# Standing the three-pass expert chunks in blocks of their own, in a two-layer diffusion backbone on one core

## The chip, the cores and the metric

One of the cores of a Trainium2 chip runs the whole program. Its engines are TensorE (PE, with its weight loads PEld), VectorE (DVE), ScalarE (ACT), GpSimd (POOL) and SyncE (SP, which here issues the loads). Each engine takes its own instructions in a fixed order and waits for the others by semaphores. The metric is device microseconds of one execution; lower is better.

## The reference, cut to what matters

Two layers work on 256 latent and 256 context tokens of width 1024. Layer 0 is a gated MLP mixer and a dense SwiGLU, layer 1 a recurrent mixer and a mixture of experts. The change touches the experts alone:

```
logits = hf @ w_router                        # 256 tokens, 8 experts
top_val, top_idx = lax.top_k(logits, 2)
probs = softmax(top_val)
combine = sum(one_hot(top_idx, 8) * probs[..., None], axis=1)
for e in range(8):
    out = out + combine[:, e:e+1] * ((silu(hf @ w_gate[e]) * (hf @ w_up[e])) @ w_down[e])
```

Here w_gate and w_up are 1024 x 3584 and w_down 3584 x 1024 for each expert, all float32: 352 MB for the eight.

## The kernel before, in words

All weights come from HBM once, in blocks of 128 x 2048 (1 MB), by one queue on SP, into 13 buffers in the expert stage. A load starts when its buffer is free, in the order in which the chunks stand in the program.

The tokens are routed on the chip, and the experts 1 to 7 are ranked by how many tokens chose them. Rank 1, 2 and 3 make lane 0, and expert 0 and the ranks 7, 6, 5, 4 make lane 1 (`moe_regions`, lines 162 to 187). An expert's hidden width of 3584 is cut into 7 chunks of 512. A chunk takes 6 blocks: two of gate, two of down (of an earlier chunk of the expert, since the down product needs the gated result) and two of up. Chunks of the lanes alternate in a fixed list.

Ranks 1 and 2 (`THREE`, line 159) are the fullest. Their chunks run in `whole` (lines 1370 to 1394), with the weights as the moving operand in three passes: each quarter of a block, a piece, is rounded on ACT (the cast, L1354), the rest is taken on DVE (the subtraction, L1355), and PE multiplies three times (L528, L529, L530). There are 24 pieces in a full chunk, so 72 matmuls, and four pairs of buffers (`whp`, `wlp`) for pieces; `prep` (lines 1363 to 1368) makes pieces ahead, four of them before the chunk begins. For the down product the hidden tile is first transposed on PE (L1379) and split by ACT and DVE (L1380, L1381). The silu stands in L1392 and the product with up in L1394.

All other chunks run in `chunk` (lines 1327 to 1347), in float32 without rounding, in an arm chosen by the number of tokens. I call these the side chunks. In such a chunk PE transposes the hidden tile (L1332), ACT copies it (L1333), PE does gate (L1314), down (L1341) and up (L1314), and ACT and DVE sum partial results in a chain (`total`, L1320 to L1324, then L1336 and L1347). Tokens of an expert beyond 128 go through the same chunk again in the over block (`over`, lines 1404 to 1417, entered by the test at L1456). When an expert is done, its rows are scattered back into the tokens (`scatter`, L1400).

The order on each engine is made by a scheduler. It may mix the instructions that stand in the program between tests. What stands inside a tested block (`tc.If`) it places as one piece. In the kernel before, the side chunks and the over blocks are such pieces, and `whole` stands outside of any (line 1443).

Of the kernel before, what the change touches and what calls it, by code (L numbers as in the profile page):

```python
# [158 lines left out]
THREE = (1, 2)  # L159
# [33 lines left out]
def region_slots(op):  # L193
    kind, r, c = op
    out = []
    for w in "gdu":
        cc = c - LAG[r] if w == "d" else c
        if 0 <= cc < NCH:
            out += [(r, cc, w, i) for i in range(2)]
    return out  # L200
# [90 lines left out]
def block_kernel(ctx, tc, xin, pos, cst, rows, wsT, adaS, adaT, wA, lruG, wr, wM, out):  # L291
# [235 lines left out]
    def mm3(o, lh, ll, rh, rl, start, stop):  # L527
        PE.matmul(o, lh, rh, start=start, stop=False)  # L528
        PE.matmul(o, lh, rl, start=False, stop=False)  # L529
        PE.matmul(o, ll, rh, start=False, stop=stop)  # L530
# [796 lines left out]
    def chunk(U, n, bt, bg, bu, yb_, raws, first, last, hd, hw, hook=None):  # L1327
        rg, rd, ru = raws
        m = P // n
        if rd:  # L1330
            for kk in range(4):
                PE.transpose(bt[:, kk * m:(kk + 1) * m], hd[0:m, kk * P:(kk + 1) * P], ident[0:m, 0:m])  # L1332
            ACT.copy(U.th[:, 0:4 * m], bt[:, 0:4 * m])  # L1333
        if rg:
            proj(bg, U.x, rg, n)
            ACT.activation(hw[0:m], total(bg, n), AF.Silu)  # L1336
        if rd:
            for kk in range(4):
                r, g = divmod(kk, n)
                for hf in range(2):  # L1340
                    PE.matmul(yb_[hf][m * g:m * g + m], U.th[:, kk * m:(kk + 1) * m], rd[hf][1][:, kk * 512:(kk + 1) * 512],  # L1341
                              start=(first and r == 0), stop=(last and r == 4 // n - 1), **tp(n, g))
        if rd and hook is not None:
            hook()
        if ru:
            proj(bu, U.x, ru, n)
            DVE.tensor_mul(hw[0:m], hw[0:m], total(bu, n))  # L1347
# [3 lines left out]
    def piece(key, kk, n):  # L1351
        raw = st.peek(key)[:, kk * 512:(kk + 1) * 512]
        wh, wl = wp[0][:, n % 4], wp[1][:, n % 4]
        ACT.copy(wh, raw)  # L1354
        DVE.tensor_tensor(out=wl, in0=raw, in1=wh.bitcast(F32), op=ALU.subtract)  # L1355
        return wh, wl
# [3 lines left out]
    def pieces(op):  # L1360
        return [(k, kk) for k in region_slots(op) for kk in range(4)]

    def prep(op, n):
        got = ahead.setdefault(op, [])
        ps = pieces(op)
        while len(got) < min(n, len(ps)):
            got.append(piece(*ps[len(got)], cnt[0]))
            cnt[0] += 1

    def whole(E, op, bt, bg, bu):  # L1370
        c = op[2]
        hw = hsel(E, c, E.hh)[1]
        prep(op, 4)
        ps = pieces(op)
        xh, xl_ = E.base.x
        yb_ = E.base.y
        if any(k[2] == "d" for k, _ in ps):
            for kk in range(4):
                PE.transpose(bt[:, kk * P:(kk + 1) * P], hw[:, kk * P:(kk + 1) * P], ident)  # L1379
            ACT.copy(thl[0], bt)  # L1380
            DVE.tensor_tensor(out=thl[1], in0=bt, in1=thl[0].bitcast(F32), op=ALU.subtract)  # L1381
        for n, ((_, _, w, i), kk) in enumerate(ps):
            wh, wl = ahead[op][n]
            kb = 4 * i + kk
            if w == "d":
                q = slice(kk * P, (kk + 1) * P)
                mm3(yb_[i], thl[0][:, q], thl[1][:, q], wh, wl, c == 1 and kk == 0, c == NCH and kk == 3)
            else:
                mm3(bg if w == "g" else bu, xh[:, kb], xl_[:, kb], wh, wl, kb == 0, kb == 7)
            prep(op, n + 5)  # L1390
            if w == "g" and kb == 7:
                ACT.activation(hw, bg, AF.Silu)  # L1392
            if w == "u" and kb == 7:
                DVE.tensor_mul(hw, hw, bu)  # L1394

    def scatter(GT, src):
        for hf in range(2):
            for t in range(2):
                b = nb[0]()
                PE.matmul(b, GT[:, t * P:(t + 1) * P], src[:, hf * 512:(hf + 1) * 512], start=True, stop=True)  # L1400
                a = acc[:, t, hf * 512:(hf + 1) * 512]
                DVE.tensor_add(a, a, b)

    def over(E, c, n, raws):
        U = E.over
        p0, p1 = bks[2 * par[0]:2 * par[0] + 2]
        first = c == LAG[E.e]
        yb_ = [p0, p1]

        def keep():  # L1410
            for hf in range(2):
                yc = U.y[:, 512 * hf:512 * hf + 512]
                if first:
                    DVE.tensor_copy(yc, yb_[hf])
                else:
                    DVE.tensor_add(yc, yc, yb_[hf])  # L1416
        chunk(U, n, p0, p1, p0, yb_, raws, True, True, *hsel(E, c, E.oh), keep)

    def hsel(E, c, hh):
        lag = LAG[E.e]  # L1420
        c += NCH * E.n
        return hh[(c - lag) % lag], hh[c % lag]

    def region(E, op, raws):
        c = op[2]
        p0, p1 = bks[2 * par[0]:2 * par[0] + 2]
        lag = LAG[E.e]
        a = (p1, p0, p1, E.base.y, raws, c == lag, c == NCH + lag - 1, *hsel(E, c, E.hh))

        def few_():  # L1430
            if E.e == 3:
                with tc.If(E.rl > 32) as c2:
                    chunk(E.base, 4, *a)
                with c2.Else():
                    chunk(E.base, 2, *a)
                return
            with tc.If(E.rv > 32) as c2:
                chunk(E.base, 2, *a)
            with c2.Else():
                chunk(E.base, 4, *a)  # L1440

        if E.e in THREE:
            whole(E, op, p1, p0, p1)
        elif E.e == 3:
            with tc.If(E.rl > 0) as c1:
                few_()
            with c1.Else():
                chunk(E.base, 1, *a)
        else:
            with tc.If(E.rv > 64) as c1:  # L1450
                chunk(E.base, 1, *a)
            with c1.Else():
                few_()
        if E.e >= 4:
            return
        with tc.If(E.ro > 0):  # L1456
            with tc.If(E.ro > 32) as c3:
                over(E, c, 1, raws)
            with c3.Else():
                over(E, c, 4, raws)  # L1460
# [3 lines left out]
    E = exps[0]  # L1464
# [65 lines left out]
    def start(E):  # L1530
        E.over = over_st[E.s, E.n % 2]
        E.oh = hu[E.s]
        E.base.y = ((y0, y1), (y2, y3))[E.s]
        gather_over(E)
# [3 lines left out]
    def yrot(E):  # L1538
        def f():
            cyc[0] += 1  # L1540
            return E.base.y[cyc[0] % 2]
        return f
    parts = {}
    runs = [o for o in regs if o[0] in "RF"]
    for kind, e, c in regs:
        if kind == "O":
            exps[e] = Expert(e, Qr)
            parts[e] = gather_parts(exps[e])
            parts[e][0]()
        elif kind == "G":  # L1550
            for f in parts[e][1:]:
                f()
            start(exps[e])
        elif kind == "S":
            E = exps[e]
            nb[0] = yrot(E)
            scatter(E.base.GT, Ys[E.s])
            if e < 4:
                with tc.If(E.ro > 0):
                    DVE.tensor_scalar(E.over.y, E.over.y, E.over.ps, None, op0=ALU.mult)  # L1560
                    scatter(E.over.GT, E.over.y)
            nb[0] = rot
        else:
            E = exps[e]
            par[0] ^= 1
            op = (kind, e, c)
            n = runs.index(op)
            if n + 1 < len(runs) and e not in THREE and runs[n + 1][1] in THREE:
                prep(runs[n + 1], 4)
            keys = region_slots(op)  # L1570
            rg, rd, ru = [[(None, st.peek(k)) for k in keys if k[2] == w] or None for w in "gdu"]
            region(E, op, (rg, rd, ru))
            rg, rd, ru = [st.take_raw([k for k in keys if k[2] == w]) for w in "gdu"]
            for r in (rg, rd, ru):
                if r:
                    st.free(r)
            if kind == "F" and c == NCH + LAG[e] - 1:
                ACT.activation(Ys[E.s][:, 0:512], E.base.y[0], AF.Copy, scale=E.base.ps)
                DVE.tensor_scalar(Ys[E.s][:, 512:1024], E.base.y[1], E.base.ps, None, op0=ALU.mult)
# [38 lines left out]
```

## Time and profile before

| | us |
|---|---|
| median of 3 runs (lowest, highest) | 1915.27 (1914.77, 1919.74) |
| the profiled execution: its own time | 1919.62 |
| its span, from the first to the last instruction | 1917.8 |
| PE busy | 1669.5 (87%) |
| DVE busy | 1063.2 (55%) |
| ACT busy | 768.6 (40%) |
| loads: 489 MB read, mean over the span | 256 GB/s |

The span has three parts. Up to about 860 us runs all but the experts, with PE busy in nearly every slice. From 895 to 1599 us the chunks of rank 1 and 2 alternate with side chunks, and PE's busy share falls to seven or eight tenths. After 1599 us rank 3 and the last ranks of lane 1 run. The profile's times come from one execution; a wait named there is put down to what released it last. "PEq" or "DVEq" with a line is the sequencer at a branch.

### The profile page before, as it was taken

What the parts mean: (1) busy time and instruction counts of PE and PEld (TensorE: products, weight loads), DVE (VectorE), ACT (ScalarE), POOL (GpSimd) and SP (SyncE); (2) the same over time, 40 slices, a digit from 0 to 9 for tenths busy, and PEclk for the clock granted to TensorE, in tenths of its full rate; (3) what the DMA queues carried; (4) which work ended last, traced back from release to release, by engine and by line L of the source; (5) the groups of instructions that cost most, each with busy time, mean ns of one, the idle gap of its engine ahead of it and who ended that gap; (6) DMA issues with size and microseconds to landing.
All of it is one profiled execution on the core that took longest, in us unless ns stands there. A gap on an engine that the chain in (4) does not pass through costs nothing. (4 is left out here: it accounts for less than half of the span.)

```text
span 1917.8 us, 23295 instructions
## 1 busy us (share of the span) xinstructions
PE 1669.5 (87%) x8528; PEld 1121.2 (58%) x8528; DVE 1063.2 (55%) x1699; ACT 768.6 (40%) x1178; POOL 19.4 (1%) x22
## 2 busy tenths in 40 slices
PE   5999999999999999976678787787787888889987
PEld 2888887988888887754344444544455454433332
DVE  3776746579774378974455555545455542222224
ACT  5523225632222268933445444425444441122221
POOL 0000001000000000010000000000000000000000
PEclk9999999999999999988899888988888999899999
DMA  8554424356764222457778868857889887979991
GB/s 348 212 184 144 164 89 149 111 185 237 279 249 169 98 87 69 168 208 308 312 317 330 328 269 325 328 232 296 350 359 392 357 342 296 410 312 382 407 413 70
DMA packets 70420, 492.92 MB, mean 257 GB/s; under 512 B 7968, under 2 KB 8160, under 8 KB 11872
## 3 DMA queue, kind: packets, MB, share of 16 engines
q1 hardware_dynamic: 70240, 490.45, 65.1%
q8 instruction: 121, 1.98, 0.4%
q14 instruction: 59, 0.48, 0.1%
HBM read 489.34 MB, written 1.08 MB: 256 GB/s over the span
## 5 line engine op out<-in xcount | busy, mean ns | idle before, releaser
L1321 DVE TENSOR_TENSOR ta__6625<-ps,ta__6625 64x512 f32<-64x512 f32 x112 | 76.5, 683 | 379.7 <-ACT ta__6625 L1320 360.3
L544 PE MATMUL ps<-hThi,wh 128*128 128x512 f32 (+1 forms) x736 | 255.6, 348 | 3.0 <-ACT hThi L395 3.0
L545 PE MATMUL ps<-hTlo,wh 128*128 128x512 f32 (+1 forms) x736 | 252.5, 344 | 1.4 <-DVE hTlo L396 1.3
L546 PE MATMUL ps<-hThi,wl 128*128 128x512 f32 (+1 forms) x736 | 253.4, 345 | 0.0
L1314 PE MATMUL ps<-raw,x 128*32 128x512 f32 (+1 forms) x1344 | 239.9, 616 | 11.4 <-issue 3.9
L1355 DVE TENSOR_TENSOR wlp<-raw,whp 128x512 fp32r<-128x512 f32 x336 | 218.7, 686 | 31.4 <-ACT whp L1354 29.2
L271 ACT CAST wh<-raw 128x2048 fp32r<-128x2048 f32 x69 | 131.6, 1910 | 228.6 <-PE ps L545 115.1
L1354 ACT CAST whp<-raw 128x512 fp32r<-128x512 f32 x336 | 196.8, 619 | 48.0 <-PE ps L530 34.6
L272 DVE TENSOR_TENSOR wl<-raw,wh 128x2048 fp32r<-128x2048 f32 x69 | 158.7, 2303 | 64.1 <-ACT wh L271 63.4
L1320 ACT COPY ta__6625<-ps 64x512 f32<-64x512 f32 x112 | 65.2, 582 | 290.2 <-PE ps L1314 268.5
L410 DVE SCALAR_TENSOR_TENSOR dj<-raw,srow 128x1024 bf16<-128x1024 f32 x128 | 156.1, 1220 | 36.5 <-DMA raw<-in_adaT_dram 33.0
L1341 PE MATMUL ps<-raw,hx 128*32 128x512 f32 (+1 forms) x896 | 152.2, 615 | 12.9 <-ACT hx L1333 12.8
L1314 PEld LDWEIGHTS ps<-raw,x 128*32 128x32 f32 (+1 forms) x1344 | 77.2, 126 | 137.9 <-issue 129.4
L544 PEld LDWEIGHTS ps<-hThi,wh 128*128 128x128 f32 x736 | 138.8, 189 | 21.2 <-ACT hThi L395 3.6
L528 PE MATMUL ps<-whp,xh 128*128 128x512 f32 x224 | 106.0, 473 | 51.8 <-ACT whp L1354 46.3
L545 PEld LDWEIGHTS ps<-hTlo,wh 128*128 128x128 f32 x736 | 138.7, 189 | 20.7 <-DVE hTlo L396 2.0
L546 PEld LDWEIGHTS ps<-hThi,wl 128*128 128x128 f32 x736 | 138.9, 189 | 18.4 <-issue 0.5
L530 PE MATMUL ps<-wh,pl 128*128 128x512 f32 x304 | 118.6, 391 | 1.0 <-DVE pl L775 1.0
L528 PE MATMUL ps<-wh,ph 128*128 128x512 f32 x304 | 119.4, 393 | 0.0
L529 PE MATMUL ps<-wl,ph 128*128 128x512 f32 x304 | 118.4, 389 | 0.0
L529 PE MATMUL ps<-wlp,xh 128*128 128x512 f32 x224 | 105.9, 473 | 13.7 <-DVE wlp L1355 13.4
L1341 PEld LDWEIGHTS ps<-raw,hx 128*32 128x32 f32 (+1 forms) x896 | 49.0, 122 | 95.9 <-issue 71.7
(355 smaller groups left out, 2310.5 us busy)
## 6 DMA issues: line engine op xcount, KB each, us to landing
raw<-in_wM_dram SPq DMA_DIRECT2D x336, 1024.0 KB, 11.6
raw<-in_wA_dram SPq DMA_DIRECT2D x69, 1024.0 KB, 4.9
raw<-in_adaT_dram SPq DMA_DIRECT2D x40, 1024.0 KB, 4.8
va<-in_adaS_dram SPq DMA_DIRECT2D x4, 1024.0 KB, 10.5
ysum<-in_xin_dram SPq DMA_DIRECT2D x4, 512.0 KB, 5.7
vb<-in_adaS_dram SPq DMA_DIRECT2D x2, 1024.0 KB, 10.2
srow<-in_adaS_dram SPq DMA_DIRECT2D x2, 1024.0 KB, 11.5
lw<-in_lruG_dram SPq DMA_DIRECT2D x8, 256.0 KB, 3.1
```

Source lines behind the costliest of these rows:

```text
L271: self.nc.scalar.copy(wh, raw)
L272: self.nc.vector.tensor_tensor(out=wl, in0=raw, in1=wh.bitcast(F32), op=ALU.subtract)
L410: DVE.scalar_tensor_tensor(j, raw[:, kk * D:(kk + 1) * D], 1.0, srow[:, vv], op0=ALU.mult, op1=ALU.mult, accum_out=adaC[l, bb // 8][:, bb ...
L528: PE.matmul(o, lh, rh, start=start, stop=False)
L529: PE.matmul(o, lh, rl, start=False, stop=False)
L544: PE.matmul(o, wh[:, r], hThi[:, kk, c0:c1], start=(kk == 0), stop=False)
L545: PE.matmul(o, wh[:, r], hTlo[:, kk, c0:c1], start=False, stop=False)
L546: PE.matmul(o, wl[:, r], hThi[:, kk, c0:c1], start=False, stop=(kk == 7))
L1314: PE.matmul(o[m * g:m * g + m], x[:, kb, 0:m], raws[kb // 4][1][:, (kb % 4) * 512:(kb % 4 + 1) * 512], start=(r == 0), stop=(r == 8 // n - ...
L1341: PE.matmul(yb_[hf][m * g:m * g + m], U.th[:, kk * m:(kk + 1) * m], rd[hf][1][:, kk * 512:(kk + 1) * 512], start=(first and r == 0), stop= ...
L1354: ACT.copy(wh, raw)
L1355: DVE.tensor_tensor(out=wl, in0=raw, in1=wh.bitcast(F32), op=ALU.subtract)
```

## The change

The call of `whole` moves into a block under the test that rank 1's or 2's overflow count is above -1. The count is never negative, so the block is always entered; the built program has no comparison for it, only an unconditional branch at its start and one at its end on each of the five engines. The first four pieces of a chunk, where they are not yet made, are now asked for in the main loop before the block, instead of in `whole`.

```diff
     def whole(E, op, bt, bg, bu):
         c = op[2]
         hw = hsel(E, c, E.hh)[1]
-        prep(op, 4)
         ps = pieces(op)
...
         if E.e in THREE:
-            whole(E, op, p1, p0, p1)
+            with tc.If(E.ro > -1):
+                whole(E, op, p1, p0, p1)
         elif E.e == 3:
...
             n = runs.index(op)
             if n + 1 < len(runs) and e not in THREE and runs[n + 1][1] in THREE:
                 prep(runs[n + 1], 4)
+            if e in THREE:
+                prep(op, 4)
             keys = region_slots(op)
```

Lines after 1373 get numbers one or two off: the transposes of `whole` are L1378 in the changed kernel, its split L1379 and L1380, its silu L1391, the scatter L1399.

On PE, around the chunk that stands between 1136 and 1180 us in the trace before (rank 1; the over block of the chunk ahead ends at the first row; `hx` holds hidden tiles, `whp` and `wlp` the two parts of a piece, `xh` and `xl` those of the tokens), the kernel before has:

```order
L1456 UNCONDITIONAL_BRANCH
L1379 MATMUL ps<-ident,hx 128x128 x4
L528 MATMUL ps<-whp,xh 128x512
L529 MATMUL ps<-wlp,xh 128x512
L530 MATMUL ps<-whp,xl__6794 128x512
...
L1450 COMPARE_AND_BRANCH
...
L1332 MATMUL ps<-ident,hx 128x32 x4
L1314 MATMUL ps<-raw,x 32x512 x8
L1341 MATMUL ps<-raw,hx 32x512 x8
L1314 MATMUL ps<-raw,x 32x512 x8
L1437 UNCONDITIONAL_BRANCH
L528 MATMUL ps<-whp,xh 128x512
```

The transposes and four triples (12 matmuls) of the three-pass chunk stand ahead of the side chunk, and the other 60 behind it. The changed kernel has on PE at the same place:

```order
L1456 UNCONDITIONAL_BRANCH
L1450 COMPARE_AND_BRANCH
...
L1332 MATMUL ps<-ident,hx 128x32 x4
L1314 MATMUL ps<-raw,x 32x512 x8
L1341 MATMUL ps<-raw,hx 32x512 x8
L1314 MATMUL ps<-raw,x 32x512 x8
L1436 UNCONDITIONAL_BRANCH
L1442 UNCONDITIONAL_BRANCH
L1378 MATMUL ps<-ident,hx 128x128 x4
L528 MATMUL ps<-whp,xh 128x512
L529 MATMUL ps<-wlp,xh 128x512
```

The side chunk follows the over block at once, and all 72 matmuls stand behind it, between the two branches of L1442. On ACT, the kernel before has at this place:

```order
L1456 UNCONDITIONAL_BRANCH
L1380 CAST thh<-ps 128x512
L1354 CAST whp<-raw 128x512 x4
L1450 COMPARE_AND_BRANCH
...
L1333 COPY hx<-ps 128x128
...
L1437 UNCONDITIONAL_BRANCH
L1354 CAST whp<-raw 128x512 x8
```

and the changed kernel:

```order
L1456 UNCONDITIONAL_BRANCH
L1354 CAST whp<-raw 128x512 x4
L1450 COMPARE_AND_BRANCH
...
L1333 COPY hx<-ps 128x128
...
L1436 UNCONDITIONAL_BRANCH
L1442 UNCONDITIONAL_BRANCH
L1379 CAST thh<-ps 128x512
L1354 CAST whp<-raw 128x512 x8
```

The four casts stay ahead of the side chunk on ACT (and the four subtractions on DVE); the split of the hidden tile moves behind it. The third place is on PE, where expert 0's rows are scattered and rank 1's chunk 3 begins. Before, the scatter's matmuls stand among those of the chunk:

```order
L528 MATMUL ps<-whp,xh 128x512
L1400 MATMUL ps<-Y_6620,GT 128x512
L529 MATMUL ps<-wlp,xh 128x512
L530 MATMUL ps<-whp,xl__6794 128x512
```

and in the changed kernel they stand ahead of it, with the test of the overflow's scatter (L1559) between:

```order
L1399 MATMUL ps<-Y_6620,GT 128x512 x4
L1559 COMPARE_AND_BRANCH
L1399 MATMUL ps<-accy,GTu_6635 128x512 x4
L1559 UNCONDITIONAL_BRANCH x2
L1442 UNCONDITIONAL_BRANCH
L1378 MATMUL ps<-ident,hx 128x128 x4
L528 MATMUL ps<-whp,xh 128x512
```

## Rows read from the trace of the kernel before

**Rows 1.** Stretches: us, then busy us of PE, PEld, DVE, ACT, POOL, clock, DMA share, GB/s.

```profile
895.00:1283.50 388.50, 297.02 (x1614) 170.18 (x1607) 204.50 (x314) 169.79 (x302) 0.00 (x0) 0.89 0.77 309
1283.50:1599.00 315.50, 251.93 (x1190) 153.97 (x1190) 164.67 (x263) 138.67 (x246) 0.00 (x0) 0.89 0.84 341
1351.70:1397.30 45.60, 37.01 (x180) 20.98 (x180) 22.96 (x36) 21.58 (x38) 0.00 (x0) 0.82 0.98 404
```

**Rows 2.** Groups by line on PE, 885 to 1600 us: busy, mean, idle before.

```profile
L528 PE MATMUL ps<-whp,xh 128*128 128x512 f32 x224 | 106.0, 473 | 51.8 <-ACT whp L1354 46.3 <-DVEq L1456 5.4
L529 PE MATMUL ps<-wlp,xh 128*128 128x512 f32 x224 | 105.9, 473 | 13.7 <-DVE wlp L1355 13.4
L1341 PE MATMUL ps<-raw,hx 128*32 128x512 f32 (+1 forms) x464 | 61.8, 618 | 9.2 <-ACT hx L1333 9.2
L1379 PE MATMUL ps<-ident,hx 128*128 128x128 f32 x56 | 10.8, 324 | 25.6 <-DVE hx L1347 8.8 <-DVE hb L1347 7.2 <-DVEq L1456 5.5
```

**Rows 3.** Timeline of PE, 1126 to 1174 us: start, length, [idle before].

```profile
1127.39 0.40 PE L528 MATMUL ps<-whp,xh 128*128 128x512 f32 x1
1127.62 0.39 PE L529 MATMUL ps<-wlp,xh 128*128 128x512 f32 x1
...
1134.59 1.89 PE L1314 MATMUL ps<-raw,xu 128*32 128x512 f32 x14
1139.36 0.74 PE L1379 MATMUL ps<-ident,hx 128*128 128x128 f32 x4 [2.88 <-DVE ta__6625 L1324]
1141.42 0.80 PE L528 MATMUL ps<-whp,xh 128*128 128x512 f32 x1 [1.32 <-ACT whp L1354]
...
1143.16 0.63 PE L528 MATMUL ps<-whp,xh 128*128 128x512 f32 x1
1143.59 0.63 PE L529 MATMUL ps<-wlp,xh 128*128 128x512 f32 x1
...
1146.91 0.43 PE L1332 MATMUL ps<-ident,hx 32*128 32x32 f32 x4
1147.27 1.92 PE L1314 MATMUL ps<-raw,x 128*32 128x512 f32 x16
...
1150.72 1.94 PE L1314 MATMUL ps<-raw,x 128*32 128x512 f32 x16
1155.36 0.49 PE L528 MATMUL ps<-whp,xh 128*128 128x512 f32 x1 [2.70 <-ACT whp L1354]
1156.75 0.77 PE L529 MATMUL ps<-wlp,xh 128*128 128x512 f32 x1 [0.89 <-DVE wlp L1355]
...
1172.25 0.43 PE L1332 MATMUL ps<-ident,hu 32*128 32x32 f32 x4
```

**Rows 4.** Timeline of ACT, 940 to 950 and 1140 to 1148 us.

```profile
946.73 2.18 ACT L1354 CAST whp<-raw 128x512 fp32r<-128x512 f32 x4 [3.76 <-DMA raw<-in_wM_dram]
...
1140.13 0.58 ACT L1380 CAST thh<-ps 128x512 fp32r<-128x512 f32 x1 [1.64 <-PE ps L1379]
1140.74 2.18 ACT L1354 CAST whp<-raw 128x512 fp32r<-128x512 f32 x4
1147.37 0.27 ACT L1333 COPY hx<-ps 128x128 f32<-128x128 f32 x1 [4.45 <-PE ps L1332]
```

**Rows 5.** Timeline of DVE, 1139 to 1144 us.

```profile
1139.25 0.68 DVE L1347 TENSOR_TENSOR hu<-hu,ta__6625 32x512 f32<-32x512 f32 x1
...
1141.39 2.50 DVE L1355 TENSOR_TENSOR wlp<-raw,whp 128x512 fp32r<-128x512 f32 x4
```

**Rows 6.** Timeline of PE, 1252 to 1262 us: two side chunks' down products.

```profile
1252.41 1.94 PE L1341 MATMUL ps<-raw,hx 128*32 128x512 f32 x16
...
1258.41 2.96 PE L1341 MATMUL ps<-raw,hx 128*32 128x512 f32 x16 [1.99 <-ACT hx L1333]
```

**Rows 7.** Waits, 885 to 1600 us: total, times, longest (PE, then SP's queue).

```profile
PE ps L1332 <- issue: 6.8, 4, 3.0
...
SPq L243 <- PEq L1456: 207.4, 14, 23.2
```

## The prediction

> **What bounds the kernel now.** I read the busy tenths of the page first: PE is nearly full in the first half and again at the end, and has seven or eight tenths where the three-pass chunks run, with the loads at eight tenths there too. So I cut that part into stretches. In the 704 us from 895 to 1599 PE is busy 549 us, which leaves 155 us in which it does nothing; the loads run at 309 and 341 GB/s, while one stretch of 45.6 us reaches 404 [rows 1]. Neither is at its limit, so PE waits for the other engines in most of it. The groups by line say at what: the first matmuls of a piece wait 51.8 us for casts and 13.7 us for subtractions, and the transposes of a three-pass chunk 25.6 us [rows 2], 91 us in sum. The timeline of one chunk shows where in it [rows 3]. The over block ahead of it ends on PE at 1136.48. The transposes start at 1139.36, after 2.88 us idle; the first matmul at 1141.42, after 1.32. The head of 12 then takes until the side chunk's first row at 1146.91, 5.5 us, since after these pauses matmuls start 0.43 us apart, against 0.23 in the chunk before: the clock is at its lower level, and the stretches show it as a mean of 0.89 [rows 1, 3]. The side chunk ends at 1152.66. Then PE stands idle for 2.70 and 0.89 us, because ACT and DVE finish the side chunk's sums before they make piece five, and the 60 remaining matmuls end at 1172.25. The chunk has PE for 35.8 us, of which 72 matmuls at 0.23 and a side chunk of 5.7 fill 22.3.
>
> **The change on such a chunk.** What is computed is the same: the same matmuls, casts, subtractions and loads. What moves is the transposes, the head of 12 and the split of the hidden tile, from ahead of the side chunk to behind it, on PE, ACT and DVE. I work it through with the durations of these rows, from 1136.48 on.
>
> The side chunk now starts at 1136.48. Its transposes and gate take 2.28 us as they do from 1146.91 to 1149.19 [rows 3], to 1138.76. Its down product needs the copy L1333, and on ACT that stands behind four casts. ACT is free at 1138.49, for L1380 starts at 1140.13 after 1.64 idle; the casts take 2.18 and the copy 0.27 [rows 4], so PE goes on at 1140.94, after 2.2 us idle. This pause is new. Down and up need the 3.5 us from 1149.19 to 1152.66, and end at 1144.4. DVE is free at 1139.93 and ends the four subtractions at about 1142.5 [rows 5], so the gate's sums start late by about 0.6 us. Before, the subtraction of piece five was there 4.09 us after the end of the side chunk (1156.75 less 1152.66); now the split of the hidden tile stands ahead of it, which adds one DVE operation of about 0.7, and with the 0.6 the piece is there 5.4 us after, at 1149.8. In that time PE does the transposes (0.6) and the head of 12, whose pieces are ready (2.8 at 0.23), so it idles 2.0 instead of 3.6. From 1149.8 on 60 matmuls at 0.23 take 13.8, to 1163.6 instead of 1172.25. **8.6 us per such chunk**: the 10.4 from 1136.48 to 1146.91 go (pauses of 2.88 and 1.32, transposes and head); the side chunk takes 2.2 more; and what follows it takes 19.2 instead of 19.6, though it holds the transposes and the head now, since these fill the pause and keep the clock up.
>
> Both ends of two unknown costs. The clock after the new pause: of two down products, one without a pause takes 1.94 us and one after 1.99 us idle takes 2.96 [rows 6]. So the pause costs between 0 and about 2.5 us more, if up and the head run at that level too; I take 1.0, the rise of that one row. The two new branches on each engine: most branches in these rows leave no gap (the side chunk at 1146.91 stands behind one, with none), and a few leave up to 3.0 us [rows 7]; I take 0, the commoner case. Below nothing neither can go, since no branch and no pause speeds anything up.
>
> **The sum.** There are eight three-pass chunks of rank 1 (to 1283.5) and eight of rank 2 (to 1599).
>
> Rank 1: five have the pauses on both sides of the head, 5 x 8.6 = 43. In one of them the cast waits 3.76 us for its load [rows 4], and the side chunk would be done earlier than its own loads land: I take 6 off. Another stands behind two side chunks, 18 loads in 51 us; at 404 GB/s a load of 1.05 MB takes 2.6 us, so 18 need 47, and 4 of the 8.6 remain: 5 off. The other three have small pauses: one gains 1; the one beside which expert 0 is scattered loses 3, since the scatter's matmuls no longer stand among those of the chunk; the last, with down alone, gains 5. Together 43 - 11 + 3 = 35.
>
> Rank 2 has no over blocks, and its chunks have the same pauses, some shorter: by the same working two of 7, three of 8.6, three of 5.5, in sum 56. Here the loads come near their limit. The stretch of 45.6 us at 404 is one of two with 18 loads in which they are nearly saturated: nothing to gain there, 17 off. The whole of rank 2 moves 315.5 us at 341 GB/s, which at 404 would take 266, so no more than 49 can go; 39 is within that, and I take 3 off for one of 12 loads whose 36 us cannot fall under 31. 36.
>
> 35 + 36 = 71; less 1.0 for the clock in the eleven chunks with the new pause, **60 us**. The span of 1917.8 becomes 1858 and the execution's own 1919.6 about 1860. That execution lies 4.4 above the median of 1915.27, so the median becomes 1855.
>
> On the queue of SP: its longest waits, 207.4 us, are for PE to pass the test of an over block [rows 7], since that releases the weight buffers. These tests come earlier by what PE gains, so the loads move with PE, and no buffer is held longer than a chunk.
>
> **Rivals.** *The loads take the gain.* The buffers are freed in bursts, one chunk at a time, so the mean of 323 GB/s may be near what 13 buffers allow; then PE reaches the next side chunk sooner and stands there, behind casts that wait for their load, as at 946.73 [rows 4]. For it: the saturated stretch. Against it: in the rows read, one wait of a cast for a load, and SP waiting for PE much longer. If the mean rises only to 335, the 704 us become 704 x 323 / 335 = 679, and 25 are kept: 1890.
>
> *Nothing comes of it.* If the pause in the side chunk is as long as the ones it replaces (casts and subtractions together, 4.7, and the clock's 2.5), a chunk keeps 3 and the scatter and loads take that: 1915. Against it: PE's down product needs the copy alone, not the subtractions.
>
> *Slower: the branches.* Each chunk puts two taken branches on PE, 32 in all, at entries where PE's queue may have run dry. Gaps of up to 3.0 us that nothing in the profile explains stand at side chunks' first rows, four of them with 6.8 in sum [rows 7]. If all 32 cost 3.0, that is 96, against 60 gained: 36 slower, 1951; it decides from 20 such gaps on. Against it: the side chunks have branches at both ends and only these four show more than a trace of it. [...]
>
> **How the numbers follow.** The forecast with its own spread (30 to 95 us gained): 0.72. The loads take most of it (10 to 30): 0.12. More than 95: 0.03. Nothing: 0.05. Slower: 0.08. The bounds: rank 1 without cuts and rank 2 at its limit of 49, without clock costs, give 43 + 3 + 49 = 95, that is 1820; clock costs of 2.5 in eleven chunks (27) and twice the cuts of 11 and 3 leave 71 - 27 - 14 = 30, that is 1885. The range that leaves less than 2 in 10 out, most of it above, takes in half of the first rival: 1818 to 1893. About 0.3%, 6 us, is what a measurement here tells from no change: faster by more 0.87, within it 0.05, slower 0.08.
>
> **What would show it.** In the changed profile the transposes L1378 have almost no idle time before them (25.6 now), the casts' waits at L528 fall under 20 us, those for subtractions at L529 stay or grow, and the down products L1341 wait 20 to 35 us for L1333 instead of 9.2. The head's matmuls stand 0.23 apart. Loads from 1283 to the end of rank 2 run above 370 GB/s. The scatter of expert 0 shows up as about 3 us lost. I am wrong if L1332 or L1314 of the side chunks wait for loads, if gaps of 2 to 3 us stand at L1442's blocks, or if the 72 matmuls run at 0.43.

## The result, and the profile after

The changed kernel takes 1843.49 us (median of 4 runs, 1843.13 to 1844.76), against 1915.39 for the kernel before beside it. The ratio is 0.9621, with a 95% interval from 0.9604 to 0.9638: 72 us less. The profiled executions differ by 76.4 in their spans (1917.8 and 1841.4), since that of before lay 4.4 above its median.

Where the time came from is in the stretches of the two ranks. Columns as in [rows 1]; the rows of after first, rank 1 and rank 2, cut at the same instructions (the L1332 that follows each rank's end):

```profile
890.78:1242.18 351.40, 284.79 (x1659) 160.30 (x1658) 204.97 (x318) 171.96 (x306) 0.00 (x0) 0.93 0.84 344
1242.18:1523.51 281.33, 234.13 (x1190) 141.59 (x1191) 163.31 (x262) 139.22 (x246) 0.00 (x0) 0.94 0.93 380
```

and of before:

```profile
889.73:1283.47 393.74, 302.25 (x1659) 172.14 (x1659) 206.01 (x317) 171.54 (x306) 0.00 (x0) 0.89 0.76 307
1283.47:1599.12 315.65, 251.96 (x1190) 154.01 (x1191) 164.68 (x263) 138.70 (x246) 0.00 (x0) 0.89 0.84 340
```

Rank 1 lost 42.3 us, rank 2 34.3, and the stretch behind them 0.8 (318.7 to 317.9), while the one ahead took 1.1 more (889.7 to 890.8). The number of matmul records is the same in each pair (1659, 1190). So the 76.7 us of the two ranks are of two kinds. PE's busy time fell by 17.5 + 17.8 = 35.3, while the granted clock rose from 0.89 to 0.93 and 0.94: the three-pass matmuls (L528 to L530) were busy 48.3 us less, the side chunks' gate, down and up products 15 more. And PE's idle time fell from 155.2 to 113.8, by 41.4. The loads rose to 344 and 380 GB/s for the same bytes.

The groups by line of PE in the same part (885 to 1524 us) answer to [rows 2]:

```profile
L528 PE MATMUL ps<-whp,xh 128*128 128x512 f32 x224 | 91.6, 409 | 3.1 <-ACT whp L1354 3.0
L529 PE MATMUL ps<-wlp,xh 128*128 128x512 f32 x224 | 90.7, 405 | 8.0 <-DVE wlp L1355 8.0
L1341 PE MATMUL ps<-raw,hx 128*32 128x512 f32 (+1 forms) x464 | 71.7, 691 | 31.1 <-ACT hx L1333 28.5 <-ACTq L1456 2.0 <-issue 0.5
L1378 PE MATMUL ps<-ident,hx 128*128 128x128 f32 x56 | 9.6, 296 | 0.5 <-DVEq L1456 0.2 <-PEq L1456 0.2
```

The 51.8 us before the first matmul of a piece are 3.1, and the 25.6 before the transposes 0.5. The side chunk's down product pays for it: 31.1 us of idle time ahead of it instead of 9.2, nearly all behind the copy L1333.

The chunk of [rows 3], on PE in the changed kernel:

```profile
1118.43 0.43 PE L1332 MATMUL ps<-ident,hx 32*128 32x32 f32 x4
1118.79 1.92 PE L1314 MATMUL ps<-raw,x 128*32 128x512 f32 x16
1123.06 1.95 PE L1341 MATMUL ps<-raw,hx 128*32 128x512 f32 x16 [2.35 <-ACT hx L1333]
...
1126.66 0.66 PE L1378 MATMUL ps<-ident,hx 128*128 128x128 f32 x4
1127.07 0.48 PE L528 MATMUL ps<-whp,xh 128*128 128x512 f32 x1
1127.39 0.40 PE L529 MATMUL ps<-wlp,xh 128*128 128x512 f32 x1
1127.62 0.41 PE L530 MATMUL ps<-whp,xl__6794 128*128 128x512 f32 x1
...
1131.56 0.50 PE L529 MATMUL ps<-wlp,xh 128*128 128x512 f32 x1 [0.87 <-DVE wlp L1355]
...
1145.39 0.43 PE L1332 MATMUL ps<-ident,hu 32*128 32x32 f32 x4
```

and ACT beside it (answers to [rows 4]):

```profile
1120.54 2.18 ACT L1354 CAST whp<-raw 128x512 fp32r<-128x512 f32 x4
1122.74 0.27 ACT L1333 COPY hx<-ps 128x128 f32<-128x128 f32 x1
```

From the side chunk's first row to the next over block's are 27.0 us, where before the chunk had PE for 35.8. There is one new pause, 2.35, with the copy behind four casts, and one of 0.87 at piece five; the head's matmuls start 0.23 apart instead of 0.43.

Two waits have grown, and both come while the loads run hard. The waits from 885 to 1524 us (total, times, longest):

```profile
PE ps L1332 <- issue: 24.0, 7, 5.6
ACT whp L1354 <- DMA raw<-in_wM_dram: 21.4, 4, 7.4
```

Casts now wait 21.4 us for their load (3.8 in one wait before, [rows 4]), and gaps before side chunks that no releaser explains went from 6.8 [rows 7] to 24.0. The longest of these, in PE's timeline:

```profile
938.11 0.63 PE L1332 MATMUL ps<-ident,hb 32*128 32x32 f32 x4 [5.62 <-issue]
```

and the DMA queues within these 5.62 us (packets, MB, share of the 16 engines):

```profile
DMA packets 324, 2.33 MB, mean 415 GB/s; under 512 B 40, under 2 KB 40, under 8 KB 40
...
q1 hardware_dynamic: 323, 2.32, 100.0%
q8 instruction: 1, 0.02, 1.1%
```

The weight queue takes 100.0% of the 16 DMA engines, at 415 GB/s, and one packet of instructions comes in between. Such packets come in six of the seven gaps, nine in 24.0 us, where the two ranks as a whole have one in 7.3 us. That the core waits there for code, beside the loads, is my reading of it; no run shows it by itself.

### The profile page after: what moved, and what is told of

It reads as the page before. It is cut to its first block, busy times and chain, and to the rows that moved or that the text cites. A ratio compares the mean times of both kernels' runs of the same rounds, so it can differ in the third digit from the quotient of the medians.

```text
span 1841.4 us, 23459 instructions
## 1 busy us (share of the span) xinstructions
PE 1637.7 (89%) x8528; PEld 1100.9 (60%) x8528; DVE 1060.0 (58%) x1699; ACT 769.6 (42%) x1178; POOL 19.4 (1%) x22
## 5 line engine op out<-in xcount | busy, mean ns | idle before, releaser
L1321 DVE TENSOR_TENSOR ta__6625<-ps,ta__6625 64x512 f32<-64x512 f32 x112 | 76.4, 682 | 321.6 <-ACT ta__6625 L1320 321.6
L1314 PE MATMUL ps<-raw,x 128*32 128x512 f32 (+1 forms) x1344 | 247.8, 636 | 6.3 <-DVEq L1296 4.2
L1354 ACT CAST whp<-raw 128x512 fp32r<-128x512 f32 x336 | 198.4, 620 | 49.2 <-DMA raw<-in_wM_dram 21.4
L1341 PE MATMUL ps<-raw,hx 128*32 128x512 f32 (+1 forms) x896 | 161.4, 651 | 34.6 <-ACT hx L1333 32.0
L410 DVE SCALAR_TENSOR_TENSOR dj<-raw,srow 128x1024 bf16<-128x1024 f32 x128 | 156.2, 1220 | 35.8 <-DMA raw<-in_adaT_dram 32.3
L1314 PEld LDWEIGHTS ps<-raw,x 128*32 128x32 f32 (+1 forms) x1344 | 79.0, 129 | 139.3 <-issue 131.2
L1341 PEld LDWEIGHTS ps<-raw,hx 128*32 128x32 f32 (+1 forms) x896 | 49.5, 126 | 124.9 <-issue 70.6
L528 PE MATMUL ps<-wh,ph 128*128 128x512 f32 x304 | 119.5, 393 | 0.0
L530 PE MATMUL ps<-wh,pl 128*128 128x512 f32 x304 | 118.7, 391 | 0.8 <-DVE pl L775 0.8
L529 PE MATMUL ps<-wl,ph 128*128 128x512 f32 x304 | 118.4, 390 | 0.0
L529 PE MATMUL ps<-wlp,xh 128*128 128x512 f32 x224 | 90.7, 405 | 8.0 <-DVE wlp L1355 8.0
L528 PE MATMUL ps<-whp,xh 128*128 128x512 f32 x224 | 91.6, 409 | 3.1 <-ACT whp L1354 3.0
```

Source lines behind the costliest of these rows:

```text
L410: DVE.scalar_tensor_tensor(j, raw[:, kk * D:(kk + 1) * D], 1.0, srow[:, vv], op0=ALU.mult, op1=ALU.mult, accum_out=adaC[l, bb // 8][:, bb ...
L1314: PE.matmul(o[m * g:m * g + m], x[:, kb, 0:m], raws[kb // 4][1][:, (kb % 4) * 512:(kb % 4 + 1) * 512], start=(r == 0), stop=(r == 8 // n - ...
```

## The experiments

Edits are against the changed kernel, unless said otherwise. Each ratio is to the kernel before, run on the same chip.

**The block around rank 1 alone.**

```diff
-            with tc.If(E.ro > -1):
+            with tc.If(E.ro > -1) if E.e == 1 else nullcontext():
```

> The block stands around the chunks of rank 1 alone; rank 2 stays as in the kernel before. Theory (each chunk gains by itself, by PE's order): rank 1's stretch loses the 42 us that it lost in the changed kernel, rank 2's keeps its 316 us; the time is about 1874 us. Rival (the loads carry what one rank gains over to the other): rank 2's stretch, now met with the loads further behind, grows by 10 us or more, and the time is 1884 us or above. Rival (the gain comes from the loads running ahead in rank 2): rank 1 alone gives under 25 us, 1890 us or above.

1873.8 us, ratio 0.9757 [0.9732, 0.9782]. The two stretches of its trace:

```profile
888.54:1241.93 353.39, 285.24 (x1659) 158.56 (x1659) 204.92 (x318) 171.91 (x306) 0.00 (x0) 0.93 0.84 342
1241.93:1561.55 319.62, 255.51 (x1191) 156.44 (x1191) 164.24 (x263) 138.35 (x246) 0.00 (x0) 0.89 0.82 336
```

Rank 1 loses 40.4 and has the clock at 0.93; rank 2 stays at 0.89 and takes 4 more than before, in an execution that lies 6.3 above its median. So rank 1 gains by itself, the clock's part too, and little is carried over by the loads. Both rivals fall.

**Transposes and split ahead again, the head behind.**

```diff
     def whole(E, op, bt, bg, bu):
...
-        if any(k[2] == "d" for k, _ in ps):
-            for kk in range(4):
-                PE.transpose(bt[:, kk * P:(kk + 1) * P], hw[:, kk * P:(kk + 1) * P], ident)
-            ACT.copy(thl[0], bt)
-            DVE.tensor_tensor(out=thl[1], in0=bt, in1=thl[0].bitcast(F32), op=ALU.subtract)
...
         if E.e in THREE:
+            if any(k[2] == "d" for k, _ in pieces(op)):
+                for kk in range(4):
+                    PE.transpose(p1[:, kk * P:(kk + 1) * P], a[8][:, kk * P:(kk + 1) * P], ident)
+                ACT.copy(thl[0], p1)
+                DVE.tensor_tensor(out=thl[1], in0=p1, in1=thl[0].bitcast(F32), op=ALU.subtract)
             with tc.If(E.ro > -1):
```

> The four transposes of a three-pass chunk and the split of the hidden tile stand ahead of the side chunk again, as in the kernel before; the head of 12 matmuls stays behind it, in the block. It tells apart which of the two moves pays. Theory (the head is what pays; by the working of the prediction): the side chunk starts some 3.6 us later again (2.9 idle, 0.7 transposes), but its pause at L1341 shrinks from 2.2 to under 1, and piece five is no longer behind the split; 1 us per chunk is lost, so about 1857 us. Rival (the pause ahead of the transposes is what pays): 3.6 us come back in each of some 13 chunks, and the lower clock after the pauses with them: 1890 us or above.

1840.24 us, ratio 0.9594 [0.9565, 0.9622]; the interval overlaps that of the changed kernel, so the transposes' place is worth nothing that can be told. The groups (the transposes are L1439 here):

```profile
L528 PE MATMUL ps<-whp,xh 128*128 128x512 f32 x224 | 91.6, 409 | 3.6 <-ACT whp L1354 3.2 <-PEq L1456 0.2
L1341 PE MATMUL ps<-raw,hx 128*32 128x512 f32 (+1 forms) x464 | 68.5, 643 | 10.2 <-ACT hx L1333 7.9 <-ACTq L1456 2.0 <-issue 0.3
L1439 PE MATMUL ps<-ident,hx 128*128 128x128 f32 x56 | 11.8, 347 | 26.7 <-DVE hx L1347 10.5 <-DVE hb L1347 7.2 <-DVEq L1456 4.7
```

The transposes wait 26.7 us again, where the kernel before had 25.6, and yet the whole gain is there: the pause at L1341 shrinks by 20.9, since ACT can make the casts while PE waits at the transposes. One pause is bought with the other. What pays is the head of 12 behind the side chunk, as the theory said; the 1 us per chunk that I expected to lose was not lost. Expert 0's scatter keeps its new place here too, so this run does not part it from the head; its matmuls waited 3.3 us less after the change (9.0 to 5.7), which is little beside 72.

**No pieces ahead, and two.** The first kernel makes the four pieces inside the block:

```diff
     def whole(E, op, bt, bg, bu):
+        prep(op, 4)
...
-            if n + 1 < len(runs) and e not in THREE and runs[n + 1][1] in THREE:
-                prep(runs[n + 1], 4)
-            if e in THREE:
-                prep(op, 4)
```

The second makes two of them ahead and two inside:

```diff
     def whole(E, op, bt, bg, bu):
+        prep(op, 4)
...
-                prep(runs[n + 1], 4)
+                prep(runs[n + 1], 2)
             if e in THREE:
-                prep(op, 4)
+                prep(op, 2)
```

> No pieces are made ahead of the side chunk: the first four casts and subtractions of a three-pass chunk stand in its block too, PE's order is that of the changed kernel. Theory: the 28.5 us of waits at L1341 fall under 8, but after a side chunk PE has only the transposes to do until the first piece is there, some 4 to 5 us, and the lower clock follows; a net loss of 1 to 2 us a chunk, 1858 to 1875 us, with the waits at L528 and L529 up from 11 us to 50 or more. Rival (the pieces ahead only delay the side chunk): 1843 us or less.

> Two pieces are made ahead of the side chunk instead of four; PE's order is that of the changed kernel. Theory (the pieces ahead cost the side chunk 0.55 us each at L1341 and save the head 0.6 to 1.2 each): between no pieces, 1867 us, and four, 1843 us: about 1852 us, with the waits at L1341 at 16 to 20 us and those at L528 and L529 at 20 to 30. Rival (two are enough to cover the way to the next piece): 1835 us or less.

None ahead: 1867.47 us, ratio 0.9724 [0.9699, 0.9749]. Two ahead: 1852.95 us, ratio 0.9678 [0.9643, 0.9714]. The groups with none:

```profile
L529 PE MATMUL ps<-wlp,xh 128*128 128x512 f32 x224 | 98.9, 442 | 10.1 <-DVE wlp L1355 10.1
L528 PE MATMUL ps<-whp,xh 128*128 128x512 f32 x224 | 97.8, 437 | 26.5 <-ACT whp L1354 26.3
L1341 PE MATMUL ps<-raw,hx 128*32 128x512 f32 (+1 forms) x464 | 68.8, 644 | 13.2 <-ACT hx L1333 10.4 <-ACTq L1457 2.0 <-issue 0.7
```

and with two:

```profile
L528 PE MATMUL ps<-whp,xh 128*128 128x512 f32 x224 | 95.8, 428 | 11.0 <-ACT whp L1354 11.0
L1341 PE MATMUL ps<-raw,hx 128*32 128x512 f32 (+1 forms) x464 | 70.5, 668 | 22.1 <-ACT hx L1333 19.9 <-ACTq L1457 2.0
```

The times lie in the order of the theory, 24 us from four to none by the medians (20 by the ratios), though its sizes were off: with none the waits at L528 and L529 came to 36.6 in these groups where I asked for 50, and L1341's behind the copy to 10.4 where I said under 8. With two, L1341's 19.9 and the 20.7 at L528 and L529 (9.7 of them at L529) are as expected. In the timeline with none, the pause at the head costs more than its length:

```profile
1131.78 0.66 PE L1379 MATMUL ps<-ident,hx 128*128 128x128 f32 x4
1135.29 0.50 PE L528 MATMUL ps<-whp,xh 128*128 128x512 f32 x1 [2.86 <-ACT whp L1354]
1136.68 0.50 PE L529 MATMUL ps<-wlp,xh 128*128 128x512 f32 x1 [0.89 <-DVE wlp L1355]
...
1138.40 0.63 PE L528 MATMUL ps<-whp,xh 128*128 128x512 f32 x1
1138.83 0.63 PE L529 MATMUL ps<-wlp,xh 128*128 128x512 f32 x1
```

After 2.86 and 0.89 us idle the matmuls start 0.43 apart, as they do after 2.70 and 0.89 at piece five before the change; in the changed kernel's head, behind transposes that follow without a pause, they start 0.23 apart. So the four pieces ahead are worth their 2.2 us at the side chunk.

**The four pieces made within the side chunk, behind its copy.** The request for the next three-pass chunk's first four pieces moves from ahead of the side chunk's arms into each arm, as `pre`:

```diff
     def chunk(U, n, bt, bg, bu, ..., hook=None, pre=None):
...
             ACT.copy(U.th[:, 0:4 * m], bt[:, 0:4 * m])
+        if pre is not None:
+            pre()
...
+        def first4():
+            ahead.pop(nxt, None)
+            cnt[0] = n0
+            prep(nxt, 4)
...
-            if n + 1 < len(runs) and e not in THREE and runs[n + 1][1] in THREE:
-                prep(runs[n + 1], 4)
```

> The first four casts and subtractions are still made beside the side chunk, but within it, behind its copy L1333 on ACT, so that its down product need not wait for them. Theory (the pause at L1341 is now the largest that is left): its 28.5 us fall under 10, and nothing else grows: 1825 us. Rival (piece five and the side chunk's sums on DVE come later by as much): 1843 us. Rival (the side chunks' arms, now longer by eight instructions in each, cost fetches): above 1850 us, with issue gaps at the side chunks' first rows well above 24 us.

1832.07 us, ratio 0.9548 [0.9528, 0.9569]: faster than both kernels, and clear of the changed kernel's interval. But the pause did not go as I said. PE's group of the down product, L1343 here:

```profile
L1343 PE MATMUL ps<-raw,hx 128*32 128x512 f32 (+1 forms) x464 | 71.1, 688 | 25.2 <-ACT hx L1333 21.8 <-ACTq L1465 2.0 <-issue 1.4
```

and ACT's timeline at one of these waits (casts are L1356):

```profile
1375.05 0.62 ACT L1356 CAST whp<-raw 128x512 fp32r<-128x512 f32 x1 [5.60 <-DMA raw<-in_wM_dram]
1375.69 0.27 ACT L1333 COPY hx<-ps 128x128 f32<-128x128 f32 x1
1375.86 1.66 ACT L1356 CAST whp<-raw 128x512 fp32r<-128x512 f32 x3
```

The scheduler still puts one of the four casts ahead of the copy, and where that cast waits 5.60 us for its load, the copy waits with it. So L1343 waits 21.8 behind the copy instead of 28.5, while the waits at L529 grew from 8.0 to 12.9. What gave the rest of the gain over the changed kernel, 11 us by the medians and 14 by the ratios, is not settled: the gaps at L1332 were 15.9 in this execution, 24.0 in that of the changed kernel.

**Both rearrangements at once** (transposes and split ahead, casts behind the copy).

> Both rearrangements at once: the transposes and the split stand ahead of the side chunk, and the first four casts and subtractions behind its copy L1333. Theory (the two save the same pause at L1341, once): as the better of the two, 1832 us, with 25 us of waits ahead of the transposes and under 12 at the down products. Rival (what each saved adds up): 1828 us or less.

1837.83 us, ratio 0.9588 [0.956, 0.9615]. The groups of the transposes (L1448) and down products:

```profile
L1343 PE MATMUL ps<-raw,hx 128*32 128x512 f32 (+1 forms) x480 | 77.7, 686 | 13.6 <-ACT hx L1333 9.1 <-issue 2.5 <-ACTq L1465 2.0
L1448 PE MATMUL ps<-ident,hx 128*128 128x128 f32 x56 | 12.2, 356 | 26.7 <-DVE hx L1349 10.5 <-DVE hb L1349 7.2 <-DVEq L1465 4.9
```

The transposes' waits are as expected; those at the down products came to 13.6, 9.1 of them behind the copy, where I said under 12. The two savings don't add up. That it is as good as the better one is not shown: it lies between them.

**More branches.** In the kernel with the transposes ahead, they stand in an always entered block of their own. The edit is against that kernel:

```diff
             if any(k[2] == "d" for k, _ in pieces(op)):
-                for kk in range(4):
+                with tc.If(E.ro > -1):
+                    for kk in range(4):
...
```

> As the kernel with the transposes ahead of the side chunk, but they and the split stand in an always entered block of their own there: 24 more taken branches on PE (as many on ACT and DVE), the order of the work otherwise all but the same. It prices the branches of such a block. Theory (their targets are the next instructions, and they cost nothing): 1838 to 1845 us, as without them, 1840. Rival (each costs the 3.0 us that the longest unexplained gap took): 24 x 3.0, 1912 us; at 0.5 us each 1852.

1845.27 us, ratio 0.9627 [0.96, 0.9654]. That is 5 us over the 1840.24 without them, with overlapping intervals. If all 5 are the branches', one costs 0.2 us; the far ends of the intervals, 0.0089 of the time, would allow 17 us, 0.7 each. (The trace has 56 transposes, so 14 such blocks; at two branches for each these would be 28 rather than 24, and 17 us would be 0.6 each.) The 3.0 of the slower rival is excluded at such a block; 0.5 is unlikely, but not excluded.

**Half of the loads, in both kernels.**

The load L243 and, as an example of the three places that read a block (L1314, L1341, L1352), the last:

```diff
-            self.nc.sync.dma_start(t, src)
+            self.nc.sync.dma_start(t[:, 0:1024], src[:, 0:1024]) if self.items[self.dma_i][1] == "own" else self.nc.sync.dma_start(t, src)
...
-        raw = st.peek(key)[:, kk * 512:(kk + 1) * 512]
+        raw = st.peek(key)[:, kk % 2 * 512:(kk % 2 + 1) * 512]
```

> The changed kernel, but of every expert weight block only the first half of its columns is loaded and used twice, so the loads of the experts move half as much; all the arithmetic stays. Theory (after the change the loads, which run at 344 and 380 GB/s in the two ranks' stretches, have begun to hold PE: the casts' four waits for a load, 21 us, and most of the 24 us of issue gaps at L1332, which stand where code is fetched beside saturated loads): the two stretches, 632.7 us together, lose 25 to 40 us. Rival (the loads hide under PE): under 10 us. The time of the whole says less, since the stretch after rank 2 gains as well: about 1800 us.

> The kernel before, with the same halved loads of the experts' weights. Theory (before the change PE waited for the order on its engines and not for loads): the two stretches, 709.4 us together, lose under 15 us, so that the change's gain with halved loads is 90 to 100 us rather than 77. Rival (the loads held the kernel before just as much): both kernels lose the same, and the gain stays at 77.

The changed kernel with half of the loads takes 1834.73 us, ratio 0.9584 [0.9546, 0.9622]; the kernel before with half of them 1830.05, ratio 0.956 [0.9522, 0.9599]. Both theories fail, and the second test did not test what I meant. With shorter loads the scheduler made another order by itself, so it seems to reckon with the length of a load. In the kernel before with half loads PE's timeline reads

```profile
1109.99 0.43 PE L1332 MATMUL ps<-ident,hx 32*128 32x32 f32 x4
...
1112.42 1.95 PE L1341 MATMUL ps<-raw,hx 128*32 128x512 f32 x16
...
1116.02 0.66 PE L1379 MATMUL ps<-ident,hx 128*128 128x128 f32 x4
1116.43 0.48 PE L528 MATMUL ps<-whp,xh 128*128 128x512 f32 x1
```

with the head behind the side chunk and no block around it. Of the twelve full chunks of both ranks, one has its head of 12 ahead of a side chunk still, and several have 1 to 6 of their matmuls there. So this run shows much of the same order reached in another way, with loads halved on top, and says nothing on what loads cost the kernel before.

In the changed kernel with half loads the order moved less, but it moved (an over block and parts of the scatter stand elsewhere on PE). The named waits, in its list of waits (columns as above), went:

```profile
PE ps L1332 <- issue: 2.7, 2, 2.6
ACT whp L1354 <- DMA raw<-in_wM_dram: 0.6, 2, 0.3
```

24.0 and 21.4 became 2.7 and 0.6, which speaks for the loads' traffic behind both, though the order moved as well. The two stretches took 353.7 and 270.4 us instead of 351.4 and 281.3, 8.6 less, where I had expected 25 to 40; that is the rival's under 10, but not by its reason, since the loads' waits did go: new waits stand in the moved scatter (13.1 before its matmuls against 4.3) and at branches. What the loads cost the changed kernel in all stays open between these 8.6 us and the sum of the waits.

## Why the prediction was right, and where its sizes were off

The mechanism was right. The forecast was 60 us off a span of 1917.8 (1855 for the median); 76.4 went (1843.49). On PE the pauses that the sum was built on went nearly whole: 51.8 to 3.1, 25.6 to 0.5 and 13.7 to 8.0, together 79.5 us. Of these 21.9 came back at the down products (9.2 to 31.1), a term that the sum had, and 17.2 in the gaps at L1332 (6.8 to 24.0), which it put at nothing. The two ranks gave 76.6, which is 16.6 more than the forecast's 60: in its terms, 7.3 more in rank 1 and the 11 that were taken off for the clock, less 1.7 in rank 2.

The sum was made chunk by chunk, so it can be held against the trace the same way. Rank 1, cut at the ends of its three-pass chunks:

| chunks of rank 1 | before | after | gained | forecast, without the clock |
|---|---|---|---|---|
| one and two (a late load in two) | 88.5 | 79.2 | 9.3 | 8.6 + 2.6 |
| three to five (scatter of expert 0 in it) | 150.0 | 140.2 | 9.8 | 1 - 3 + 8.6 |
| six, the worked one | 44.1 | 35.2 | 8.8 | 8.6 |
| seven, with two side chunks | 51.3 | 43.6 | 7.8 | 3.6 |
| eight, and to the end | 59.8 | 53.2 | 6.6 | 5 |
| sum | 393.7 | 351.4 | 42.3 | 35 |

- **8.6 us per worked chunk**: 8.8. Its parts hold too: the new pause 2.35 for 2.2, the chunk 27.0 for 27.1 us. Piece five came sooner than I had it, 0.87 idle for 2.0, and the pass through the other 60 matmuls was no faster than forecast.
- **The clock, 1.0 in eleven chunks**: near in sum, wrong in place. The side chunks' gate, up and down products were busy 195.9 us in both stretches before and 210.9 after, 15 more. But in chunks six and seven nothing of it was paid; the clock stood at 1.00 there, in their stretches of the changed kernel (columns as above):

```profile
1110.23:1145.46 35.23, 30.32 (x181) 17.74 (x182) 24.52 (x38) 21.53 (x38) 0.00 (x0) 1.00 0.88 360
1145.46:1189.01 43.55, 36.20 (x233) 19.83 (x234) 27.93 (x43) 24.74 (x44) 0.00 (x0) 1.00 0.94 385
```

It is paid where long gaps and waits for loads stand: after 5.62 us idle at 938 the gate took 3.64 us, and after 6.52 at 1389 the down product 3.67, both at a granted clock of 0.50, against 1.92 and 1.95 in chunk six at 1.00.
- **The new pause, 2.2 in eleven chunks**: right in sum, by luck. The 28.5 us that L1341 waits for the copy lie within the 20 to 35 that I named, but only a few of its waits are the pause that I worked out, as the 2.35 above. Four stand behind casts that wait for a load, 2.29, 0.96, 6.52 and

```profile
1342.62 3.41 PE L1341 MATMUL ps<-raw,hx 128*32 128x512 f32 x16 [3.66 <-ACT hx L1333]
```

together 13.4. One of 3.22 was there before the change (3.24), one of 5.68, at 1085.40, comes where two side chunks follow each other, and the other seven are 1.22 and less.
- **The cut for 18 loads, the step that was mis-sized**: 5 off in chunk seven of rank 1, where it was 0.8. I took the chunk's own 18 loads at 404 GB/s, 47 us, as a floor. The chunk took 43.55 at 385 GB/s, so only 16.8 MB, 16 loads, arrived in it: the loads of the other blocks that it reads had come before it began. Over a longer stretch the same cut was nearly right. Of rank 2's two chunks with 18 loads I said that nothing could be gained; together they gained 2.7. Their stretches after:

```profile
1296.27:1334.92 38.65, 32.64 (x180) 17.83 (x180) 23.36 (x36) 21.52 (x38) 0.00 (x0) 0.96 0.98 400
1366.69:1421.30 54.61, 39.98 (x219) 24.40 (x218) 25.33 (x40) 22.80 (x40) 0.00 (x0) 0.84 0.97 400
```

These took 48.5 and 47.5 before. The first gained 9.9 us, and the second gave 7.2 back, with a gap of 5.36 ahead of its first side chunk and this wait for a load, in ACT's timeline:

```profile
1386.38 2.18 ACT L1354 CAST whp<-raw 128x512 fp32r<-128x512 f32 x4 [4.18 <-DMA raw<-in_wM_dram]
1388.58 0.27 ACT L1333 COPY hx<-ps 128x128 f32<-128x128 f32 x1
```

- **The scatter, 3 lost**: this does not show. Its second half moved from chunk five into chunk four, which took 7.3 us longer, while five took 14.0 less; together they gained 6.7 where 8.6 - 3 was forecast.
- **Rank 2, 36**: 34.3 with the clock in it. If rank 1's five chunks are among the eleven, 6 of the clock's 11 are rank 2's, and the forecast for it is 30, so 4 more than forecast.
- **Branches, 0**: no gap at the entries of the 14 new blocks that begin with transposes (0.5 us in all ahead of L1378), and 0.2 by the medians for each added one in the experiment. Behind the blocks' ends it is less clean. Gaps of 2 to 3 us at L1442's blocks were a sign that I am wrong, and behind the first block there is one:

```profile
921.03 3.64 PE L1314 MATMUL ps<-raw,xu 128*32 128x512 f32 x32 [2.75 <-issue]
```

The kernel before had 0.78 there; all nine kernels with rank 1's blocks have 2.3 to 2.8, with halved loads too, so I put 1.5 to 2 us down to this block. Three of the seven gaps at L1332 also follow a block's end (1.80, 5.36 and 5.07), with the test L1456 between, which the kernel before has too. For the 5.36, at 1372.05, the runs tell the two apart: ahead of the same side chunk all eleven kernels have a gap, and it goes with the loads within it. It is 2.2 to 2.8 us at 107 to 162 GB/s (the kernel before, that with blocks in rank 1 alone, and both with halved loads), 3.3 at 299, 3.8 to 4.5 at 368 to 383 (three) and 5.3 to 5.4 at 413 to 419 (three). One of the four short ones stands behind a block, three do not. So in these runs its length goes with the loads, and not with a block's branch ahead of it. The gaps that the slower rival was built on are real, and grew from 6.8 to 24.0 (I had overlooked one of 3.55, ahead of L1314 at 1040.33, in the kernel before), but not at the branches that it charged.
- **The rival of the loads**: it had PE standing behind casts that wait for loads, as at 1386.38 above. It came true at four places, 21.4 us of ACT's time and 13.4 of PE's, not as the bound: rank 2's mean rose to 380 GB/s, above the 370 that I asked for.
- **A sign that was wrong**: I said that the waits for subtractions at L529 stay or grow; they fell from 13.7 to 8.0. The wait at piece five stays (0.87 for 0.89 in the worked chunk), but most of the shorter ones at other pieces are gone.

## What to carry to other kernels

Where an engine has a part of its work ready early and a part that comes late, put the ready part into the pause ahead of the late one: 12 matmuls moved behind a side chunk were worth most of the pauses around them (91.1 us ahead of L528, L529 and the transposes in [rows 2], 11.6 in the changed kernel) and a rise of the mean clock from 0.89 to 0.93 and 0.94. A scheduler that orders by its own estimate of loads can be held to an order by a block that is always entered, here at a cost of some 2 us; a change of load sizes changed that order too, so it is no clean test of what loads cost. Load limits are to be reckoned over as many chunks as the buffers reach, not chunk by chunk: here 16 loads arrived within a chunk that read 18.

## What was not expected of the hardware

Gaps of up to 5.6 us stood ahead of side chunks while the load queue was full (seven, 24.0 us, with 404 to 432 GB/s in each); with the loads halved, two with 2.7, though the instruction packets were as many (56 and 31 on their two queues in the two ranks). At the one place where all eleven kernels have such a gap, it grew with the loads, from 2.2 us at 107 GB/s to 5.4 at 419. An instruction packet came within it in the seven kernels with 299 GB/s or more, in the other four none; so the packets go with the long gaps. That code is what PE waits for in these is not shown, and what the 2.2 us of a gap without a packet are stays open. And here a pause did not decide alone whether the clock fell: the down product after 2.35 us idle took 1.95 us, like one without a pause, and so did one after 3.22 (at 1040.82), both at a granted clock of 1.00, while in [rows 6] one after 1.99 us idle took 2.96, at 0.63, and after 6.52 us (at 1388.89) 3.67, at 0.50.
